# Two banks for value products, filler tied to them, and a new order of pools in the running streams' stage

## The chip, the cores and the metric

The kernel runs on one core of one Trainium2 chip, in one launch. The metric is the device time of that launch in microseconds (us); a profiled execution gives the trace. The engines run side by side, each in its own fixed order: PE (TensorE, matmuls and transposes), ACT (ScalarE), DVE (VectorE), POOL (GpSimd), and SP, which issues the DMA transfers.

## The reference

One inference step of a one-layer streaming encoder, for one prompt of 1024 frames with 16 meta rows ahead of it, and for 8 running streams of 16 new frames each, over shared weights. Attention with 16 heads of 64 and a state-space branch run in parallel, are merged by gates, and a convolutional feed-forward layer follows. The attention is "stick-breaking", and it is what the changed stage computes:

```python
def stick_breaking(q, k, v, q_pos, k_pos):
    z = jnp.einsum('bqhd,bshd->bhqs', q, k).astype(jnp.float32) * (SB_HEAD_DIM ** -0.5)
    reach = k_pos[None, :] < q_pos[:, None]
    log_beta = jax.nn.log_sigmoid(z)
    log_keep = jnp.where(reach, jax.nn.log_sigmoid(-z), 0.0)
    later = lax.cumsum(log_keep, axis=3, reverse=True) - log_keep
    w = jnp.where(reach, jnp.exp(log_beta + later), 0.0)
    return jnp.einsum('bhqs,bshd->bqhd', w.astype(v.dtype), v)
```

A running stream attends to 272 cached positions (16 meta rows and 256 past frames) and its own 16. All is float32.

## The kernel before, in words

Activations lie transposed, channels on partitions. A float32 product is made of three matmuls on numbers split into a high and a low part (high x high, high x low, low x high); the split is a cast on ACT and a subtraction on DVE. The stages run one after another: norm and projections, the state-space branch, the prompt's attention (`phase_att`), the running streams' attention (`phase_smp`, the stage that changes), the merge, the feed-forward layer.

*Prompt attention.* `head` (L678) runs once per head, 0 to 15. Per head, SP loads the keys' halves `KH` and `KL` (L686, L687) and the queries `QS` (L688, L689) from tiles in memory; each of these names is a ring of two buffers, so the loads of a head can go out while the one before it is at work. PE makes the scores (z, L707 and L710), ACT the sigmoid, DVE the scan, PE transposes the weights and multiplies them with the values (L731, L732), and L739 and L743 finish and store.

*The two first rows.* Queries 0 and 1 of the prompt see at most 16 keys. `first_queries` (L746) does them for all heads at once, from a load of its own (L752 to L755), with small matmuls at L767 and L784, at the beginning of `phase_smp`, in slots of that stage's rings.

*The running streams.* `sample_att` (L790) has 8 streams of two halves (8 heads each): 16 iterations. Ahead of them it loads queries (`qhs`, `qls`), key extensions (`kxh`, `kxl`, 16 transfers, L801) and the last cached rows (`last`, L807). In an iteration: 8 transposes of the cached keys into two banks of `pk`, split into `Ksh` and `Ksl`; POOL puts the new keys and the queries of the stream beside them (L848, L851; the queries in block-diagonal tiles `qdh` and `qdl`, of which there are two sets, used in turn); 12 matmuls make the scores z (L867, L870, L871); ACT makes the sigmoid (L873), POOL the masking (L874) and the complement (L876), DVE the scan (L877) and the products with what is kept (L880, L881); 3 transposes turn the weights, which are split into `wTh` and `wTl`; 9 matmuls (L890 to L892) multiply them with the values (`Vsh`, `Vsl`, and `V3h`, `V3l` for the last rows) into the bank `o`; ACT copies that to `od` (L894); 4 transposes turn it back into a bank `pd`, and ACT copies it out (L902).

*The eight accumulation banks* of that stage: two for the projections (`mm`), two `pk`, one `z`, two `wT` (weights and output transposes in turn), one `o`.

*Filler.* Projection blocks that nothing waits for until the merge are kept back in a list, `fill`: queries, keys and values of later heads and the 16 gate blocks (three tiles of 24 matmuls, 72 in a block; L115, L118, L119). `paced` (L954) ties the first matmul of each tile of a block to a *mark*, a matmul of the stage that has to be issued ahead of it on PE. In the prompt's attention the marks are the scores of every other block of queries; in the stage they are the first z matmul of each iteration. Of the 9 blocks that are left when attention ends, `RESERVE` are kept for the beginning of the merge.

*Order.* Memory pools are entered in a written order, each at the address that follows the one before, so a pool's place in the list decides which pools of the earlier stage lay there, and a tile's first writer waits for the last user of that space. The order of instructions on each engine is set by the framework's list scheduler when the program is built; the engines then run it as it stands, and a semaphore holds an instruction until what it needs is there.

## Time and profile before

| what | before |
|---|---|
| median of 3 runs | 3051.93 us (3051.7 to 3055.76) |
| profiled execution | 3054.39 us, its span 3052.7 us |
| mean granted clock of PE | 0.985 |
| PE busy | 2942.7 us (96%) |
| DVE, ACT, POOL busy | 1803.7 us (59%), 1167.4 us (38%), 632.9 us (21%) |
| prompt attention, about | 900 to 1520 us |
| first z matmul of the streams' stage | 1535.08 us |
| its last output transposes | 1714.44 us |

Times inside a trace are counted from the start of its span. A matmul's row gives its whole duration, and the next one begins before it ends: rates are read from the distances between starts. "Granted clock" is the share of full speed that TensorE was given.

### The profile page before, as it was taken

How to read it: one execution, taken by the hardware profiler on the slowest of the kernel's cores; microseconds unless marked ns; L12 is line 12 of the kernel's file. 1: busy time of each engine (PE TensorE's matmuls, PEld its weight loads, DVE VectorE, ACT ScalarE, POOL GpSimd, SP SyncE). 2: the span in 40 equal slices, each digit the busy share in tenths (PEclk: the TensorE clock that was granted, in tenths of full speed). 3: DMA queues.
4: the chain of work that ended last, by engine and by line, in shares of the span. 5: the costliest groups of instructions: out<-in, count | busy, mean ns of one | idle time of the engine just before them, and what ended most of it. 6: DMA issues, size and time to landing. Idle time of an engine off the chain costs nothing. (4 is left out here: it accounts for less than half of the span.)

```text
span 3052.7 us, 45429 instructions
## 1 busy us (share of the span) xinstructions
PE 2942.7 (96%) x17349; PEld 2795.2 (92%) x17349; DVE 1803.7 (59%) x2945; ACT 1167.4 (38%) x2294; POOL 632.9 (21%) x979
## 2 busy tenths in 40 slices
PE   7999999989998999999899999999999999999998
PEld 6997988979978999999789899999999999999997
DVE  6567677677675777777634441345755454545447
ACT  6432423324234555544434320214534242424245
POOL 0024133142232333333324000002201010101014
PEclk9999999999999999999999999999999999999999
DMA  5435345254465555553444462546211111111113
GB/s 186 110 88 147 106 128 159 79 133 128 129 180 152 167 144 140 161 139 103 78 132 150 140 198 90 149 114 181 80 47 43 43 43 43 43 40 39 43 43 118
DMA packets 445498, 338.46 MB, mean 111 GB/s; under 512 B 43991, under 2 KB 421155, under 8 KB 445279
## 3 DMA queue, kind: packets, MB, share of 16 engines
q1 hardware_dynamic: 445279, 335.54, 38.7%
q8 instruction: 137, 2.24, 0.3%
q14 instruction: 82, 0.67, 0.1%
HBM read 244.31 MB, written 91.15 MB: 110 GB/s over the span
## 5 line engine op out<-in xcount | busy, mean ns | idle before, releaser
L115 PE MATMUL mm<-sh,wh 128*128 128x384 f32 (+3 forms) x2520 | 871.5, 346 | 12.5 <-ACT sh L930 4.4
L118 PE MATMUL mm<-sl,wh 128*128 128x384 f32 (+3 forms) x2520 | 871.0, 346 | 2.4 <-DVE sl L931 1.2
L119 PE MATMUL mm<-sh,wl 128*128 128x384 f32 (+3 forms) x2520 | 867.3, 344 | 0.0
L115 PEld LDWEIGHTS mm<-sh,wh 128*128 128x128 f32 (+1 forms) x2520 | 476.9, 189 | 28.0 <-issue 6.6
L118 PEld LDWEIGHTS mm<-sl,wh 128*128 128x128 f32 (+1 forms) x2520 | 477.7, 190 | 13.2 <-issue 7.0
L119 PEld LDWEIGHTS mm<-sh,wl 128*128 128x128 f32 (+1 forms) x2520 | 477.3, 189 | 7.6 <-issue 5.8
L115 PE MATMUL mm<-ph,wh 128*128 128x386 f32 x1248 | 424.7, 341 | 2.7 <-ACT ph L97 2.0
L118 PE MATMUL mm<-pl,wh 128*128 128x386 f32 x1248 | 424.8, 341 | 0.0
L119 PE MATMUL mm<-ph,wl 128*128 128x386 f32 x1248 | 422.6, 339 | 0.2 <-DVE wl L106 0.2
L106 DVE TENSOR_TENSOR wl<-wf,wh 128x1024 fp32r<-128x1024 f32 (+2 forms) x205 | 255.3, 1246 | 279.0 <-ACT wh L105 278.7
L105 ACT CAST wh<-wf 128x1024 fp32r<-128x1024 f32 (+2 forms) x205 | 212.5, 1037 | 481.4 <-PE mm L118 450.4
L1139 DVE SCALAR_TENSOR_TENSOR acc<-fx,cwf,acc 128x256 f32<-128x256 f32 (+1 forms) x352 | 170.7, 515 | 154.1 <-ACT acc L1137 150.1
L115 PEld LDWEIGHTS mm<-ph,wh 128*128 128x128 f32 x1248 | 236.3, 189 | 3.9 <-ACT ph L97 2.3
L119 PEld LDWEIGHTS mm<-ph,wl 128*128 128x128 f32 x1248 | 236.4, 189 | 0.9 <-DVE wl L106 0.5
L118 PEld LDWEIGHTS mm<-pl,wh 128*128 128x128 f32 x1248 | 235.3, 189 | 1.8
L674 DVE TENSOR_TENSOR_SCAN keep<-keep 128x144 f32<-128x144 f32 (+7 forms) x128 | 179.9, 1408 | 57.5 <-POOL keep L673 56.9
L115 PE MATMUL mm<-ah,wh 128*128 128x384 f32 x528 | 179.9, 341 | 0.0
L119 PE MATMUL mm<-ah,wl 128*128 128x384 f32 x528 | 179.3, 340 | 0.0
L118 PE MATMUL mm<-al,wh 128*128 128x384 f32 x528 | 178.7, 338 | 0.0
L1066 POOL TENSOR_TENSOR sq<-sq,sq 128x386 f32<-128x386 f32 (+1 forms) x42 | 60.2, 1433 | 468.1 <-ACT sq L1065 456.6
L98 DVE TENSOR_TENSOR wTl<-wT,wTh 128x512 fp32r<-128x512 f32 (+3 forms) x176 | 103.0, 602 | 81.2 <-ACT wTh L97 80.4
L1164 DVE TENSOR_TENSOR h<-mm,h 128x384 f32<-128x384 f32 x144 | 79.7, 555 | 119.8 <-PE mm L119 119.5
(324 smaller groups left out, 4579.0 us busy)
## 6 DMA issues: line engine op xcount, KB each, us to landing
wf<-in_w_in SPq DMA_DIRECT2D x80, 512.0 KB
wf<-in_w_up SPq DMA_DIRECT2D x44, 512.0 KB
t<-s_ac SPq DMA_DIRECT2D x36, 512.0 KB
wf<-in_w_down SPq DMA_DIRECT2D x28, 512.0 KB
wf<-in_w_out SPq DMA_DIRECT2D x24, 512.0 KB
s_y<-x SPq DMA_DIRECT2D x16, 577.0 KB
yt<-s_y SPq DMA_DIRECT2D x16, 577.0 KB
KH<-s_kh SPq DMA_DIRECT2D x32, 260.0 KB
```

What stands on the lines that cost most here:

```text
L98: nc.vector.tensor_tensor(out=l, in0=x, in1=h.bitcast(F32), op=ALU.subtract)
L105: nc.scalar.copy(wh, wf)
L106: nc.vector.tensor_tensor(out=wl, in0=wf, in1=wh.bitcast(F32), op=ALU.subtract)
L115: i = nc.tensor.matmul(p, wh[:, k, :], mh[:, c:c + w], start=s, stop=False)
L118: nc.tensor.matmul(p, wh[:, k, :], ml[:, c:c + w], start=False, stop=False)
L119: nc.tensor.matmul(p, wl[:, k, :], mh[:, c:c + w], start=False, stop=e)
L674: nc.vector.tensor_tensor_scan(out=K[:, ::-1], data0=K[:, ::-1], data1=K[:, ::-1], initial=1.0, op0=ALU.mult, op1=ALU.min)
L1066: nc.gpsimd.tensor_tensor(out=acc[:, :w], in0=acc[:, :w], in1=sq, op=ALU.add)
L1139: nc.vector.scalar_tensor_tensor(out=op, in0=src(q), scalar=w(q), in1=op, op0=ALU.mult, op1=ALU.add)
L1164: self.nc.vector.tensor_tensor(out=h, in0=p, in1=h, op=ALU.add)
```

## The change

1. `RESERVE` is 2 in place of 3: one gate block moves from the merge into the streams' stage.
2. A mark in the stage is the first matmul of the value products in place of the first z matmul.
3. `wT` has one bank in place of two, `o` two in place of one, and the output transposes `pd` take their bank from the ring `pk`.
4. `first_queries` runs in `phase_att`, ahead of head 15, in slots of the rings QS, KH and KL.
5. The pools of the stage are entered in another order, and `norm_rows` (a small sum over rows for the state-space norm) runs ahead of `sample_att`.

```diff
@@ -44,7 +44,7 @@
 PAIRS_AT_START = 1
 PAIRS_AFTER_GROUP = {3: (1,)}
 RATE = 1.17
-RESERVE = 3
+RESERVE = 2
 SAMPLE_AFTER = (2, 4, 6, 8)
 FFN_GROUP = 4
 XW = 3 + TP + 19 * NB
@@ -746,15 +746,15 @@
     def first_queries(self):
 
         nc, ap, pa = self.nc, self.ap, self.pa
-        x = self.tile(ap, [128, 4, 288], F32R, 'Ksh').bitcast(F32).rearrange("p a b -> p (a b)")[:, :288]
+        x = self.tile(ap, [128, TP - T0], F32R, 'QS').bitcast(F32)[:, :288]
         x = x.rearrange("p (i j t) -> p i j t", i=2, j=8)
         for i, (qs, ks) in enumerate(((self.s_qh, self.s_kh), (self.s_ql, self.s_kl))):
             nc.sync.dma_start(x[:, i, :, 0:2], qs[:, 0:2].rearrange("(j p) t -> p j t", p=128))
             nc.sync.dma_start(x[:, i, :, 2:18], ks[:, 0:16].rearrange("(j p) t -> p j t", p=128))
-        v = self.tile(ap, [128, 2, 512], F32R, 'Vsh').bitcast(F32)[:16].rearrange("p a (j c) -> p (a j) c", c=128)
+        v = self.tile(ap, [128, TP], F32R, 'KH').bitcast(F32)[:16, :1024].rearrange("p (j c) -> p j c", c=128)
         nc.sync.dma_start(v, self.s_v[:, 0:16].rearrange("j t c -> t j c"))
         nc.vector.tensor_tensor(out=x[:, 0], in0=x[:, 0], in1=x[:, 1], op=ALU.add)
-        Q = self.tile(ap, [128, 512], F32, 'last', bufs=2)[:, :256].rearrange("p (j c) -> p j c", c=32)
+        Q = self.tile(ap, [128, TP], F32R, 'KL').bitcast(F32)[:, :256].rearrange("p (j c) -> p j c", c=32)
         nc.gpsimd.memset(Q, 0.0)
 
         def diagonal(t, e):
@@ -762,7 +762,7 @@
             return bass.AP(d.tensor, d.offset, [d.ap[0], (34, 8), (16, 2)])
         for e in range(2):
             nc.gpsimd.tensor_copy(diagonal(Q.rearrange("p j c -> p (j c)"), e), x[64 * e:64 * e + 64, 0, :, 0:2])
-        ps = self.tile(pa, [128, 512], F32, 'z')
+        ps = self.tile(pa, [128, 512], F32, 'z', bufs=2)
         for j in range(8):
             nc.tensor.matmul(ps[:32, :16], Q[:, j], x[:, 0, j, 2:18], start=(j == 0), stop=(j == 7))
         B = self.tile(ap, [32, 2, 16], F32, 'fb', bufs=1)
@@ -779,7 +779,7 @@
         self.T_(pt[:16, :32], B)
         w = self.tile(ap, [16, 32], F32, 'fw', bufs=1)
         nc.scalar.copy(w, pt[:16, :32])
-        po = self.tile(pa, [128, 512], F32, 'o')
+        po = self.tile(pa, [128, 512], F32, 'o', bufs=2)
         for j in range(8):
             nc.tensor.matmul(po[:, 32 * j:32 * j + 32], v[:, j], w, start=True, stop=True)
         out = self.tile(ap, [128, 8, 2], F32, 'fo', bufs=1)
@@ -864,9 +864,7 @@
                 z = ps[:, 0:288]
                 for j in range(4):
                     qh, ql = (Q[x][:, 128 * j:128 * j + 128] for x in range(2))
-                    mk = nc.tensor.matmul(z, qh, Kh[:, j], start=(j == 0), stop=False)
-                    if j == 0:
-                        marks.append(mk)
+                    nc.tensor.matmul(z, qh, Kh[:, j], start=(j == 0), stop=False)
                     nc.tensor.matmul(z, qh, Kl[:, j], start=False, stop=False)
                     nc.tensor.matmul(z, ql, Kh[:, j], start=False, stop=(j == 3))
                 B = self.tile(ap, [128, 288], F32, 'beta')
@@ -879,20 +877,22 @@
                 w = w3[hf][:, 96 - 32 * (b % 4):224 - 32 * (b % 4)]
                 nc.vector.tensor_tensor(out=w3[hf][:, 96:127], in0=B[:, 256:287], in1=K[:, 257:288], op=ALU.mult)
                 nc.vector.tensor_tensor(out=B[:, :256], in0=B[:, :256], in1=K[:, 1:257], op=ALU.mult)
-                pt = self.tile(pa, [128, 512], F32, 'wT', bufs=2)
+                pt = self.tile(pa, [128, 512], F32, 'wT')
                 for i, x in enumerate((B[:, 0:128], B[:, 128:256], w)):
                     self.T_(pt[:, 128 * i:128 * i + 128], x)
                 wh, wl = (self.tile(ap, [128, 3, 128], F32R, n) for n in ('wTh', 'wTl'))
                 self.split(wh, wl, pt[:, 0:384].rearrange("p (i c) -> p i c", c=128))
-                po = self.tile(pa, [128, 512], F32, 'o')
+                po = self.tile(pa, [128, 512], F32, 'o', bufs=2)
                 vs = [(Vh[:, 0], Vl[:, 0]), (Vh[:, 1], Vl[:, 1]), V3[hf]]
                 for i, (vh, vl) in enumerate(vs):
-                    nc.tensor.matmul(po, wh[:, i], vh, start=(i == 0), stop=False)
+                    mk = nc.tensor.matmul(po, wh[:, i], vh, start=(i == 0), stop=False)
+                    if i == 0:
+                        marks.append(mk)
                     nc.tensor.matmul(po, wh[:, i], vl, start=False, stop=False)
                     nc.tensor.matmul(po, wl[:, i], vh, start=False, stop=(i == 2))
                 od = self.tile(ap, [128, 512], F32, 'od', bufs=1)
                 nc.scalar.copy(od, po)
-                pd = self.tile(pa, [128, 512], F32, 'wT', bufs=2)
+                pd = self.tile(pa, [128, 512], F32, 'pk', bufs=2)
                 for j in range(4):
                     self.T_(pd[:, 128 * j:128 * j + 128], od[:, 128 * j:128 * j + 128])
                 for e in range(2):
@@ -962,7 +962,7 @@
     def phase_att(self, right, rx):
         with ExitStack() as c1:
             self.ap = {n: self.pool(c1, "att_" + n, 2) for n in (
-                'wTh', 'wTl', 'wf32', 'att', 'vf', 'KH', 'KL', 'QS', 'VV', 'keep', *(f'beta{i}' for i in range(8)))}
+                'wTh', 'wTl', 'wf32', 'att', 'vf', 'KH', 'KL', 'QS', 'VV', 'keep', *(f'beta{i}' for i in range(8)), 'fb', 'fw', 'fo')}
             self.pa = self.pool(c1, "att_ps", 1, space=PSUM)
             first = PAIRS_AT_START + sum(len(v) for v in PAIRS_AFTER_GROUP.values())
             self.fill = [b for p in range(first, 8) for b in self.qkv(p, self.pa, 'o')]
@@ -974,6 +974,8 @@
                 self.nc.sync.dma_start(v[:, 0:8], vs[0:1024].rearrange("(j t) d -> t j d", t=128))
                 self.nc.sync.dma_start(v[:16, 8], vs[1024:TP])
                 for e in range(2):
+                    if p == 7 and e == 1:
+                        self.first_queries()
                     marks += self.head(2 * p + e, v[:, :, 64 * e:64 * e + 64])
                     done = self.paced(marks, done, RATE)
                     if p + e == 0:
@@ -985,16 +987,15 @@
 
     def phase_smp(self):
         with ExitStack() as c2:
-            mp = self.stp = self.pool(c2, "mixst", 3)
+
             self.ap = {n: self.pool(c2, "smpa_" + n, 2) for n in (
-                'aout', 'od', 'wTh', 'wTl', 'keep', 'beta', 'v', 'r', 'newton', 'qdh0', 'qhs', 'qls', 'kxh', 'kxl',
-                'last', 'V3h', 'V3l', 'qdl0', 'qdh1', 'qdl1', 'Ksh', 'Ksl', 'Vsh', 'Vsl',
-                'w30', 'w31', 'fb', 'fw', 'fo')}
+                'kxh', 'kxl', 'qhs', 'qls', 'qdh0', 'qdl0', 'qdh1', 'qdl1', 'Ksh', 'Ksl', 'last', 'V3h', 'V3l', 'v', 'r', 'newton',
+                'beta', 'keep', 'Vsh', 'Vsl', 'w30', 'w31', 'wTh', 'wTl', 'od', 'aout')}
+            self.stp = self.pool(c2, "mixst", 3)
             self.pa = self.pool(c2, "smp_ps", 1, space=PSUM)
             rest, self.fill = self.fill[len(self.fill) - RESERVE:], self.fill[:len(self.fill) - RESERVE]
-            self.first_queries()
+            self.norm_rows(self.ap)
             self.sample_att(3 * len(self.fill) / 16)
-            self.norm_rows(self.ap)
             assert not self.fill
             self.fill = rest
```

Line numbers in the profile shift a little: the z matmuls' second and third lines are L868 and L869 in the changed kernel, the first of the value products L888.

What this does to the order is seen at three places. The first is PE in the stage, before, between two iterations: z of one, weights and output of the ones before it, products.

```order
L135 MATMUL pk_16866<-ident_60,ck_16854 128x128 x4
L135 MATMUL wT_16520<-ident_60,od_16518 128x128 x4
L135 MATMUL wT_16579<-ident_60,beta_16571 128x128 x2
L135 MATMUL wT_16579<-ident_60,w_2936_16001 128x128
...
L867 MATMUL z_16806<-Ksh_16779,qdh_2932_15993 128x288
L870 MATMUL z_16806<-Ksl_16780,qdh_2932_15993 128x288
L871 MATMUL z_16806<-Ksh_16779,qdl_2933_15994 128x288
L135 MATMUL pk_16873<-ident_60,ck_16854 128x128 x4
L890 MATMUL o_16587<-Vsh_16553,wTh_16583 128x512
L891 MATMUL o_16587<-Vsl_16554,wTh_16583 128x512
L892 MATMUL o_16587<-Vsh_16553,wTl_16584 128x512
```

The rows of z in two groups, `pk` of the next keys and `wT` of earlier outputs and weights lie between each other: scores and keys of later iterations (z_16806, pk_16873) stand ahead of the products of an earlier one (o_16587).

The same engine with the change, from the end of one iteration's scores to its products, and from these to the next one's scores:

```order
L868 MATMUL z_16247<-Ksl_16221,qdh_2938_16011 128x288
L869 MATMUL z_16247<-Ksh_16220,qdl_2939_16012 128x288
L135 MATMUL wT_16268<-ident_60,beta_16260 128x128 x2
L135 MATMUL wT_16268<-ident_60,w_2941_16018 128x128
L888 MATMUL o_16276<-Vsh_16242,wTh_16272 128x512
L891 MATMUL o_16276<-Vsl_16243,wTh_16272 128x512
L892 MATMUL o_16276<-Vsh_16242,wTl_16273 128x512
```

```order
L892 MATMUL o_16276<-V3h_16043,wTl_16273 128x512
L135 MATMUL pk_16288<-ident_60,od_16286 128x128 x4
L135 MATMUL pk_16307<-ident_60,ck_16295 128x128 x4
L135 MATMUL pk_16314<-ident_60,ck_16295 128x128 x4
L867 MATMUL z_16326<-Ksh_16299,qdh_2936_16009 128x288
```

The weights now follow their own scores directly, the products the weights; the output transposes (pk_16288) stand ahead of the next keys, which take the same ring, and the next scores behind both. Gate blocks stand in 7 of the 16 iterations, all of them behind the first products (17 matmuls between the second and the third product, 25 ahead of the output transposes, 30 behind these, or nearly so).

The second place is POOL in the stage, with the change:

```order
L874 TENSOR_SCALAR keep_16342<-beta_16339 128x288
L862 TENSOR_TENSOR Vsl_16570<-ck_16545,Vsh_16569 128x512
L851 CAST qdh_2938_16011<-qhs_15943 64x4x16 x2
L848 CAST Ksl_16717<-kxl_15948 128x4x32
L848 CAST Ksh_16716<-kxh_15947 128x4x32
L851 CAST qdl_2939_16012<-qls_15944 64x4x16 x2
L872 TENSOR_TENSOR beta_16508<-beta_16508,cst_67 128x16
L874 TENSOR_SCALAR keep_16511<-beta_16508 128x288
```

The copies for a later iteration (L851, L848), into tiles that the scores at work read, stand ahead of this iteration's masking (L872, which was L874).

The third is SP, where head 15's loads go out, before:

```order
L743 DMA s_att_86<-att_14435 64x512
L686 DMA KH_15414<-s_kh_76 64x1040
L687 DMA KL_15415<-s_kl_77 64x1040
L659 DMA s_gate_87<-st_14967 128x386
L686 DMA KH_15414<-s_kh_76 64x1040
L687 DMA KL_15415<-s_kl_77 64x1040
L688 DMA QS_15416<-s_qh_79 64x1026
L689 DMA QS_15416<-s_ql_80 64x1026
```

and with the change:

```order
L743 DMA s_att_86<-att_14885 64x512
L659 DMA s_gate_87<-st_15392 128x384
L686 DMA KH_15467<-s_kh_76 64x1040
L687 DMA KL_15468<-s_kl_77 64x1040
L686 DMA KH_15467<-s_kh_76 64x1040
L687 DMA KL_15468<-s_kl_77 64x1040
L659 DMA s_gate_87<-st_15420 128x386
L688 DMA QS_15469<-s_qh_79 64x1026
L689 DMA QS_15469<-s_ql_80 64x1026
```

The loads of KH, KL and QS stand behind a later attention store (att_14885, two stores on from att_14435); and they take the buffers that head 14 uses, since the two first rows now have the others.

## The prediction

> **What bounds the kernel now.** The first view is the page's table of busy time, with its slices and its costliest groups:
>
> ```profile
> PE 2942.7 (96%) x17349; PEld 2795.2 (92%) x17349; DVE 1803.7 (59%) x2945; ACT 1167.4 (38%) x2294; POOL 632.9 (21%) x979
> L115 PE MATMUL mm<-sh,wh 128*128 128x384 f32 (+3 forms) x2520 | 871.5, 346 | 12.5 <-ACT sh L930 4.4
> ```
>
> TensorE is busy for 96% of the span, and no other engine for more than 59%. So time can be gained only where PE idles or runs at a lower clock, and lost wherever PE is made to wait. The second view is the table of windows around the streams' stage (after the window its length, then busy us and instructions of PE, PEld, DVE, ACT and POOL, then the granted clock, DMA share and GB/s):
>
> ```profile
> 1500.00:1520.00 20.00, 13.43 (x58) 9.75 (x59) 11.03 (x14) 5.68 (x11) 4.27 (x7) 0.74 0.90 113
> 1520.00:1540.00 20.00, 11.95 (x62) 11.09 (x62) 6.87 (x21) 8.46 (x20) 7.98 (x17) 0.59 0.47 105
> 1560.00:1700.00 140.00, 135.16 (x836) 127.85 (x835) 59.54 (x101) 62.12 (x127) 50.64 (x113) 1.00 0.42 133
> 1700.00:1720.00 20.00, 15.22 (x71) 11.76 (x70) 4.08 (x6) 7.28 (x15) 1.77 (x3) 0.91 0.31 78
> 1720.00:1740.00 20.00, 20.00 (x115) 20.00 (x114) 11.21 (x9) 7.44 (x9) 0.00 (x0) 1.00 0.66 194
> ```
>
> Two places are slack: the 40 us across the border from prompt attention to the stage, and the stage's last 20 us. Between them PE works 97% of the time at full clock: there the stage is as short as its PE work. The last row also gives the filler's price: 115 matmuls in 20 us, 0.174 us each, so 12.5 us for a gate block of 72. The third view is PE's timeline at the two ends of the stage (start, duration, instruction, idle time before it and what ended that):
>
> ```profile
> 1520.00 0.68 PE L767 MATMUL z<-Ksh,last 128*32 128x16 f32 x16
> 1528.33 0.20 PE L135 MATMUL wT<-ident,fb 32*16 32x32 f32 x1 [6.93 <-DVE fb L777]
> 1528.80 3.62 PE L784 MATMUL o<-fw,Vsh 16*128 16x32 f32 x16 [0.27 <-ACT fw L781]
> 1532.35 1.11 PE L135 MATMUL pk<-ident,last 128*128 128x128 f32 x4
> 1535.08 0.58 PE L867 MATMUL z<-Ksh,qdh 128*128 128x288 f32 x1 [0.77 <-ACT Ksh L97]
> ...
> 1714.44 0.66 PE L135 MATMUL wT<-ident,od 128*128 128x128 f32 x4 [1.69 <-ACT od L894]
> ```
>
> The two first rows take from 1520.00 to 1532.35, 12.35 us. The stage proper runs from the first z at 1535.08 to the end of the last od transposes at 1715.1: 180 us for 16 iterations and 6 gate blocks.
>
> **The change: the order of PE.** In the new order each iteration runs alone: key transposes, z, weight transposes, value products, output transposes, and only then the next one's. Before, the next iteration's keys and z stood between a z and its weights, or filler did. Now nothing does, because the output transposes have moved to the ring `pk` of the keys: an iteration takes three turns of two slots, so the second key transposes of the next one wait for these output transposes and their copies. The filler cannot step in, since it waits for the first value product. So the latency of the chain counts, which the end of the stage shows today, where filler has run out:
>
> ```profile
> 1698.67 0.30 PE L867 MATMUL z<-Ksh,qdh 128*128 128x288 f32 x1
> 1698.95 0.29 PE L871 MATMUL z<-Ksh,qdl 128*128 128x288 f32 x1
> 1699.73 0.40 PE L890 MATMUL o<-Vsh,wTh 128*128 128x512 f32 x1
> 1700.89 0.39 PE L892 MATMUL o<-V3h,wTl 128*128 128x512 f32 x1
> 1702.26 0.66 PE L135 MATMUL wT<-ident,od 128*128 128x128 f32 x4 [0.98 <-ACT od L894]
> 1702.97 0.27 PE L135 MATMUL wT<-ident,w 128*128 128x128 f32 x1
> 1703.93 0.50 PE L890 MATMUL o<-Vsh,wTh 128*128 128x512 f32 x1 [0.69 <-ACT wTh L97]
> 1705.11 0.63 PE L890 MATMUL o<-Vsh,wTh 128*128 128x512 f32 x1
> 1707.25 0.63 PE L892 MATMUL o<-V3h,wTl 128*128 128x512 f32 x1
> ```
>
> An iteration's eight key transposes in the full flow of the stage:
>
> ```profile
> 1552.38 1.04 PE L135 MATMUL pk<-ident,ck 128*128 128x128 f32 x8
> ```
>
> The rest of the chain, on the other engines:
>
> ```profile
> 1699.32 0.41 ACT L873 ACTIVATE beta<-z 128x288 f32<-128x288 f32 x1 [1.53 <-issue]
> 1702.95 0.42 ACT L902 COPY aout<-wT 64x64 f32<-64x64 f32 x2 [0.75 <-PE wT L135]
> 1699.81 0.22 POOL L874 TENSOR_TENSOR beta<-beta,cst 128x16 f32<-128x16 f32 x1 [1.71 <-ACT beta L873]
> 1700.12 0.43 POOL L876 TENSOR_SCALAR keep<-beta 128x288 f32<-128x288 f32 x1
> 1700.59 0.76 DVE L877 TENSOR_TENSOR_SCAN keep<-keep 128x288 f32<-128x288 f32 x1 [0.81 <-POOL keep L876]
> 1701.56 0.42 DVE L881 TENSOR_TENSOR beta<-beta,keep 128x256 f32<-128x256 f32 x1
> ```
>
> Z ends at 1699.24; sigmoid, masking, complement, scan and product end at 1701.98. The gap from z to the weights is 2.8 us. Then 0.7 us from the weights to the first product (the cast), 1.0 us from the last product to the output transposes (the copy), 0.75 us to the copies that free `pk`, and 0.75 us for the keys' cast ahead of z (0.77 at 1535.08): gaps of 6.0 us. PE's own work is 9 products at 0.23 (five steps in 1.16 us), 12 z at 0.14, 8 + 4 + 3 transposes at 0.12 (eight in 1.04, with the last one's end): 5.6 us, of which the first four key transposes (0.5) fall into a gap. 6.0 + 5.1 makes a **period of about 11.0 us** without filler, where the stage today hides all but PE's own work.
>
> POOL can lengthen it. In its new order six copies for a later iteration stand ahead of the masking, and they wait for this very z's last matmuls:
>
> ```profile
> L851 POOL CAST qdh<-qhs 64x64 fp32r<-64x64 f32 x28 | 7.6, 273 | 36.2 <-PE z L870 35.4
> L848 POOL CAST Ksh<-kxh 128x128 fp32r<-128x128 f32 x14 | 4.2, 302 | 0.9 <-PE z L871 0.9
> ```
>
> Two of the first and one of the second for the high halves, and as many for the low ones, are 1.7 us, of which the sigmoid and its hand-over (0.6) run beside: at most 1.1 us more, period 12.1 us. I take half, 11.6.
>
> Seven iterations carry a gate block behind the first value products, which fills the gap to the output transposes and that to the copies (1.75 us): a block adds 12.5 - 1.75 = 10.8 us. Sum of the stage at full clock: 16 x 11.6 + 7 x 10.8 = 186 + 76 = 262 us; bounds 252 and 270.
>
> **The clock.** The trace shows how little rest lowers it (windows of 2 us, the clock in the third column from the end):
>
> ```profile
> 1504.00:1506.00 2.00, 0.00 (x0) 0.00 (x0) 1.90 (x2) 0.00 (x0) 0.00 (x0) 1.00 0.97 91
> 1506.00:1508.00 2.00, 0.85 (x3) 0.45 (x3) 1.41 (x3) 0.80 (x2) 1.09 (x3) 0.61 1.11 104
> 1508.00:1510.00 2.00, 2.00 (x5) 1.26 (x6) 1.10 (x2) 0.27 (x1) 0.00 (x0) 0.50 0.96 106
> 1540.00:1542.00 2.00, 2.00 (x14) 1.97 (x13) 0.69 (x1) 0.86 (x2) 0.00 (x0) 0.86 0.61 208
> ```
>
> A rest of some 3 us before 1506.7 halves it, and after 1535.08 it takes 5 us of matmuls to come back (0.86 in the window from 1540). At 1705.11 to 1707.25 the products stand 0.43 us apart (five steps in 2.14), nearly double. In the new order the stretch from z to the first product is 2.8 + 0.3 + 0.7 = 3.8 us with 0.3 us of work in it (4.4 with half of the copies), and an iteration without filler has nowhere 5 us of unbroken work. So the nine without filler should run at half clock: products +1.75, z +0.55, transposes +0.85, by these rows +3.1 us each, 28 us. Those with a block start it at half clock: z, keys, weights and the first filler, about +1.5 us, 10 us. Stage 262 + 38 = 300 us; bounds 252 (no penalty, no copies) and 270 + 46 = 316 (all sixteen lose somewhat more). The change to today's 180: **+120 us**, from +72 to +136.
>
> The Trainium skill, TensorE: Matmul & The Clock Gate, section Part 1: The HAM clock gate, has the array at half clock after one idle window of about 3.4 us and back after one busy window of that length, the windows running free. By it about half of the 38 us would be lost. The rows from 1703.93 to 1707.25 speak for the dearer reading: nearly half clock there with no idle of 3.4 us ahead.
>
> **The change at head 15.** The two first rows now take slots of the rings of QS, KH and KL, so the loads for head 15 wait until head 14's last z has read its own:
>
> ```profile
> 1430.55 0.46 SPq L686 DMA_DIRECT2D KH<-s_kh  x1
> 1434.10 0.59 SPq L689 DMA_DIRECT2D QS<-s_ql  x1
> 1468.72 0.32 PE L707 MATMUL z<-KH,QS 128*128 128x344 f32 x1
> 1469.92 0.28 PE L707 MATMUL z<-KH,QS 128*128 128x256 f32 x1
> DMA packets 1573, 2.36 MB, mean 197 GB/s; under 512 B 133, under 2 KB 1127, under 8 KB 1572
> ```
>
> Today they are issued 35 us before use. Now they go out after 1469.2, with head 15's first z due at 1469.92. They are 4 x 260 + 2 x 256.5 KB = 1.55 MB, 7.9 us at the 197 GB/s measured over 1429 to 1441 (the last row), 9 us with the issues: z near 1478. Some 3 us of other PE work stand there, so PE loses 5 us, and 2 more for the rows' own matmuls at full clock: +7. SP's order also has those loads ahead of gate stores and a weight load, which the same 7 us delay; filler already loaded covers that.
>
> **The change at the border.** The gap of 12.35 us for the two first rows goes; that is the gain. Against it: the key extensions and query loads wait for the end of the attention's tail, and SP then issues 8 of the former, 2 queries, 16 key tails and 16 value tails, at 0.46 to 0.60 each (rows of the loads above) some 20 us in a row; the filler now waits for the first value product, one chain later. From 1520.00 the first z stood 15.1 us off, and filler began behind it; I estimate 17 us to z and 25 to the first product. Net from -12 (gain kept whole) to +10; I take +2.
>
> **Sum of squares moved ahead.** norm_rows' few instructions fall beside the tail; on ACT and DVE they cost 0 to 1.6 us there, inside the bounds above. The merge begins with one gate block less: -12.5 us, if the loads behind it are not waited for instead. ACT's scaled rows already end 4.4 us of PE's waits (the group of L115); a shorter cover gives back 0 to 12.5. I take 6.
>
> **Sum.** 3054.39 (the profiled execution, 2.46 above the median shown) + 120 + 7 + 2 - 6 = 3177; less 2 for the median: 3175. Between the outer bounds: low 3052 + 72 + 5 - 12 - 12.5 = 3104; high 3052 + 136 + 8 + 10 = 3206.
>
> **Rivals.** (1a) The chain is serial, but a gap of 3.8 us lowers the clock only now and then: half of the 38 us, 3156. For it: the 3 us that halved it before 1506.7 were wholly idle, and here 0.3 us of work stands in the gap. (1b) The clock holds throughout: 3137. For it: blocks of 12.5 us of full work in 7 of 16 iterations. Against both: the slow products from 1703.93 on. (2) The order costs nothing in the stage, because what I read as a wait is covered; then only the edges count: 7 + 2 - 6, and 12.5 for the added block, 3067. Against it: no instruction stands between a z and its weights in the new order, and PE runs in order. (3) **Not slower**: the gap at the border is gained whole and the period is short. With the block (7 x 10.8 = 76), +7 and -6 and -12.35, today's time is reached at 16 P = 180 + 11 - 76, P = 7.2 us; below that it is faster. At 5.0 us, PE's own work, the time would be 3052 - (7.2 - 5.0) x 16 = 3017, at 6.5 some 3041; between them 3030. It would take z to weights in under 1 us or z ahead of the products; the sigmoid, scan and product alone take 1.6.
>
> **Numbers.** Forecast 0.45; rival 1a 0.22, 1b 0.17; rival 2 0.07; rival 3 0.05; above the high bound (the stage's loads late besides) 0.04. Range 3108 to 3206, which takes in 1a and 1b and leaves out the last three, and what lies at the edges of the first three. What the measurement can tell from no change is 0.2%, 6 us: faster 0.04, same 0.03 (rival 3 near its point, or rival 2 with the outer gains), slower 0.93.
>
> **What would show it.** Right: from first z to the last od transposes about 300 us; PE's idle put before `wT<-ident,beta` (waiting for DVE's L881 product) of 2.5 to 4 us, sixteen times; clock 0.5 to 0.7 in windows without filler; no filler between a z and its products; head 15's first z waiting for the DMA of KH, KL or QS some 5 us. Wrong: a stage under 230 us; idle put before filler rows instead (then weight loads are late); a clock of 1.0 throughout (1b); a merge that starts with PE idle over 6 us (then the reserve was its cover).

## The result and the profile after

The changed kernel takes 3190.08 us (median of 4 runs, 3188.48 to 3195.04) where the kernel before takes 3051.81 us beside it: a ratio of 1.0456, with a 95% interval of 1.0443 to 1.0469. It is 138 us slower; 3175 was forecast, with a range of 3108 to 3206. The profiled execution has a span of 3189.7 us, 137.0 us more than before's 3052.7, and the clock granted over it is 0.964 where it was 0.985.

The page of the changed kernel, busy time and slices:

```profile
PE 2994.4 (94%) x17349; PEld 2826.8 (89%) x17349; DVE 1805.1 (57%) x2945; ACT 1170.6 (37%) x2294; POOL 630.1 (20%) x979
PE   7999999999999999998677789999999999999998
...
PEclk9999999999999999998778789999999999999999
```

PE runs the same 17349 matmuls, for 52 us longer. The loss lies in one place: slices 19 to 23 (counted from 0), where both PE and its clock sink, are the streams' stage. The windows of the stage, from its first z to its last od transposes, say how (after the window its length, busy time and instructions of PE, PEld, DVE, ACT and POOL, the clock, DMA share, GB/s). Before:

```profile
1535.00:1715.00 180.00, 169.18 (x1005) 157.55 (x1006) 72.60 (x123) 77.35 (x156) 57.76 (x133) 0.98 0.42 131
```

and with the change:

```profile
1545.60:1868.50 322.90, 232.56 (x1077) 199.04 (x1078) 75.71 (x125) 82.53 (x160) 56.16 (x132) 0.80 0.27 82
```

The stage grew from 180 to 322.9 us, by 143. PE's idle time in it went from 10.8 to 90.3 us, which is 79.5 of these; its busy time rose by 63.4, of which 12.5 are the added gate block and the rest is work at a lower clock, 0.80 where it was 0.98. Who waits there is told by the view of waits over the same stretch of the changed kernel (total, times, longest, in us):

```profile
POOL qdh L851 <- PE z L868: 104.3, 14, 13.2
PE wT L135 <- DVE beta L879: 60.6, 16, 4.4
DVE keep L875 <- POOL keep L874: 57.0, 16, 4.4
```

PE's transposes of the weights wait for DVE's product in all 16 iterations, 60.6 us in all. In the same view of the kernel before, over its stage, this wait does not stand at all, and the longest of PE's waits is

```profile
PE wT L135 <- ACT od L894: 3.4, 3, 1.7
```

PE's timeline in the changed kernel: the first weights of the stage, and the last two iterations, the first of them behind a block (rows that only go on with the same tiles are left out):

```profile
1554.84 0.66 PE L135 MATMUL wT<-ident,beta 128*128 128x128 f32 x2 [4.38 <-DVE beta L879]
...
1842.23 0.37 PE L867 MATMUL z<-Ksh,qdh 128*128 128x288 f32 x1 [1.04 <-ACT Ksh L97]
1845.24 0.44 PE L869 MATMUL z<-Ksh,qdl 128*128 128x288 f32 x1
1848.57 0.66 PE L135 MATMUL wT<-ident,beta 128*128 128x128 f32 x2 [2.88 <-DVE beta L879]
1850.01 0.80 PE L888 MATMUL o<-Vsh,wTh 128*128 128x512 f32 x1 [0.57 <-ACT wTh L97]
1854.89 0.66 PE L135 MATMUL pk<-ident,od 128*128 128x128 f32 x4 [0.73 <-ACT od L894]
1855.39 1.33 PE L135 MATMUL pk<-ident,ck 128*128 128x128 f32 x8
1856.77 0.37 PE L867 MATMUL z<-Ksh,qdh 128*128 128x288 f32 x1
1858.84 0.29 PE L869 MATMUL z<-Ksh,qdl 128*128 128x288 f32 x1
1862.02 0.41 PE L135 MATMUL wT<-ident,beta 128*128 128x128 f32 x2 [2.89 <-DVE beta L879]
1867.37 1.12 PE L135 MATMUL pk<-ident,od 128*128 128x128 f32 x4 [0.73 <-ACT od L894]
```

Each iteration is a chain with nothing of another in it. From weights to weights an iteration without filler takes 14.5 us on average, one with a block 27.3 (eight and seven of them make the 307.2 us from 1554.84 to 1862.02).

At the border, four of PE's rows in the changed kernel:

```profile
1476.27 0.58 PE L707 MATMUL z<-KH,QS 128*128 128x256 f32 x1 [1.57 <-DMA QS<-s_ql]
1526.29 0.64 PE L739 MATMUL o<-wf,VV 128*128 128x144 f32 x4
1539.26 1.09 PE L135 MATMUL pk<-ident,last 128*128 128x128 f32 x4 [12.34 <-DMA last<-in_cache_k]
1545.62 0.58 PE L867 MATMUL z<-Ksh,qdh 128*128 128x288 f32 x1 [0.77 <-ACT Ksh L97]
```

Head 15's first scores come at 1476.27, 6.35 us later than before; the tail ends at 1526.9 (before 1520.1) and the first z is 10.5 us later. The 12.35 us that the two first rows held PE are replaced by a wait of 12.34 us for the last cached rows, and behind it PE waits 2.56 us more for the values of these rows. From the stage's end to that of the span it is 1321.2 us where it was 1337.6. So 6.9 + 3.6 + 142.9 - 16.4 = 137.0.

### The profile page after: what moved, and what is told of

It reads as the page before. It is cut to its first block, busy times and chain, and to the rows that moved or that the text cites. A ratio compares the mean times of both kernels' runs of the same rounds, so it can differ in the third digit from the quotient of the medians.

```text
span 3189.7 us, 45521 instructions
## 1 busy us (share of the span) xinstructions
PE 2994.4 (94%) x17349; PEld 2826.8 (89%) x17349; DVE 1805.1 (57%) x2945; ACT 1170.6 (37%) x2294; POOL 630.1 (20%) x979
## 4 chain that ended last, share of the span: by engine, by line
PE 74%; DMA 7%; DVE 7%; issue 6%; POOL 3%; ACT 2%; SPq 1%; POOLq 0%; ACTq 0%; DVEq 0%
PE mm L115 21%; PE mm L118 20%; PE mm L119 20%; PE wT L135 3%; DMA t<-s_ac 2%; DMA yt<-s_y 1%; PE z L707 1%; DVE t L458 1%; DMA zf<-s_z 1%; PE o L732 1%; PE z L710 1%; PE o L731 1%; PE yd L472 1%; PE tp L135 1%; POOL Vsl L862 1%
## 5 line engine op out<-in xcount | busy, mean ns | idle before, releaser
L115 PE MATMUL mm<-sh,wh 128*128 128x384 f32 (+3 forms) x2520 | 872.5, 347 | 7.6 <-DVE st L549 2.3
L115 PEld LDWEIGHTS mm<-sh,wh 128*128 128x128 f32 (+1 forms) x2520 | 479.3, 190 | 23.1 <-issue 6.6
L115 PE MATMUL mm<-ph,wh 128*128 128x386 f32 x1248 | 425.2, 341 | 2.0 <-ACT ph L97 2.0
L115 PEld LDWEIGHTS mm<-ph,wh 128*128 128x128 f32 x1248 | 236.8, 190 | 2.9 <-ACT ph L97 2.3
L135 PE MATMUL wT<-ident,beta 128*128 128x128 f32 x736 | 123.6, 282 | 65.8 <-DVE beta L879 60.6
L115 PE MATMUL mm<-ah,wh 128*128 128x384 f32 x528 | 179.8, 340 | 0.0
L135 PEld LDWEIGHTS wT<-ident,beta 128*128 128x128 f32 x736 | 94.4, 147 | 81.5 <-issue 62.2
```

What stands on the lines that cost most here:

```text
L115: i = nc.tensor.matmul(p, wh[:, k, :], mh[:, c:c + w], start=s, stop=False)
L135: self.nc.tensor.transpose(out, in_, self.ident[:k, :k])
```

## The experiments

The theory (A): the output transposes in the ring of the keys make the iterations run one at a time. The rival (B): the marks do it, since filler tied to the value products cannot fill the gap ahead of them. Four kernels separate the two edits, each alone on the kernel before, and each undone in the changed one. These four, and the last two kernels of this section, were run once each; runs of the kernel before lie between 3046 and 3057 us. The lengths of stages are read from one trace of each kernel.

**The banks alone.** On the kernel before:

```diff
-                pt = self.tile(pa, [128, 512], F32, 'wT', bufs=2)
+                pt = self.tile(pa, [128, 512], F32, 'wT')
-                po = self.tile(pa, [128, 512], F32, 'o')
+                po = self.tile(pa, [128, 512], F32, 'o', bufs=2)
-                pd = self.tile(pa, [128, 512], F32, 'wT', bufs=2)
+                pd = self.tile(pa, [128, 512], F32, 'pk', bufs=2)
```

> The kernel before with the third edit alone: one bank for the weights' transposes, two for the value products, the output transposes in the ring of the key transposes. Theory A (the ring makes each iteration run alone): PE's order is serial; the ten iterations without filler take some 14 us each as in the changed kernel, the six with a block some 20, since its 45 matmuls stand in the gap from the scores to the weights: stage 260 us where it was 180, time 3125 to 3145. Theory B (the marks, not the banks, open the gap): the time stays within 10 us of before.

Measured: 3133.74 us beside 3052.75, stage 263.2 us. PE's first rows in the view of waits:

```profile
PE wT L135 <- DVE beta L881: 37.1, 10, 3.9
PE pk L135 <- ACT od L894: 13.4, 16, 1.0
```

The gap is open in exactly the 10 iterations that have no block; in the other 6 the filler closes it. This edit alone makes 83 us of the stage's loss.

**The marks alone.** On the kernel before, `marks.append` moved from the first z matmul to the first value product.

> The kernel before with the second edit alone: filler is tied to the first value product. Theory A: the next scores still run ahead and fill the gap, so the stage stays under 205 us and the time rises by 5 to 25 us, 3057 to 3077. Theory B (the marks open the gap): the stage is over 260 us, the time over 3130.

Measured: 3063.41 us beside 3052.75, stage 188.4 us. With the rings as before, the next keys and scores run ahead and fill the gap, so filler is hardly missed.

**The banks undone** in the changed kernel (`wT` two, `o` one, `pd` in `wT`):

> The changed kernel with the third edit undone (two banks for weights and output transposes in turn, one for value products); all else as changed. Theory A: nearly all of the stage's loss goes; stage 193 (its 180 and a block of 12.5) to 215 us, time 3050 to 3080. Theory B: the stage stays over 290 us, time over 3155.

Measured: 3068.74 us, stage 201.2 us. Of 143 us of loss in the stage, 122 go.

**The marks undone** in the changed kernel:

> The changed kernel with the second edit undone: filler is tied to the first z matmul again. Theory A: the order stays serial; seven gaps are filled by 45 matmuls of a block, nine stay open; 9 x 14.5 + 7 x 20 = 270 us for the stage where it is 323, time some 3135 (3125 to 3150). Theory B: the stage returns to some 193 us, the time to 3060.

Measured: 3131.77 us, stage 268.5 us: 54 us go, since seven gaps are filled again. The four results agree with A, and rule out B as the whole cause. But the two edits cost more together than the sum of both: banks alone +83 us in the stage, marks alone +8, both +143, of which 12.5 are the added block. What closes a gap today is either the next scores or filler; the one edit takes away the first, the other the second.

**What is left without the two.** The changed kernel with both undone:

> The changed kernel with the second and third edits undone (banks and marks as before); what is left is the moved gate block, the two first rows ahead of head 15, and the pools. Theory A (the two undone edits made the stage's loss): stage 190 to 197 us, first z as late as in the changed kernel (+10 us), the rest 16 us shorter; 3050 to 3066. Theory B (pools and late head also hold the stage back, by POOL's copies or late loads): stage over 205, time over 3070.

Measured: 3056.58 us, ratio to before 1.0015 (1.0006 to 1.0024), stage 188.5 us, a little under the range of theory A. It is 8.5 us longer than before with 12.5 us of work more in it.

**Two banks without the keys' ring.** The changed kernel with marks as before and

```diff
-                pd = self.tile(pa, [128, 512], F32, 'pk', bufs=2)
+                pd = self.tile(pa, [128, 512], F32, 'o', bufs=2)
```

> The changed kernel with the marks at the first z again and the output transposes in the ring of the value products (two banks) in place of the keys' ring. Theory A: with the keys' ring free the next scores run ahead, so two banks for products are no harm: stage 188 to 200 us, 3048 to 3066. Theory B (sharing any ring with the output transposes makes the iterations run alone): stage over 240, time over 3110.

Measured: 3053.21 us, ratio 1.0002 (0.9992 to 1.0011), stage 187.6 us. The kernel with the marks undone differs from this one in the ring of `pd` alone, and its stage takes 268.5 us, 81 more. So neither two banks for the products nor a shared ring as such is the fault: the output transposes stand at the end of an iteration and the keys at its beginning, and sharing a ring between these two ties the beginning of the next iteration to the end of this one.

**The two first rows alone**, moved ahead of head 15, on the kernel before:

> The kernel before with the fourth edit alone: the two first rows ahead of head 15. Theory A: head 15 begins 6 to 8 us late since its loads wait for head 14's last scores, and the 12 us between the tail and the keys' tails are saved only in part: first z between -6 and +5 us, time 3046 to 3058. Theory B (the gap is gained whole): first z 12 us earlier, time under 3043.

Measured: 3048.75 us, ratio 0.9989 (0.9979 to 0.9998), the only one of these kernels that beats the kernel before, by a tenth of a per cent, with the end of the interval close to 1. First z 5.5 us later, just past the edge of what theory A allows, but the stage is 173.8 us, 6.2 less, and the rest 3.0 less. Why the stage is shorter is not shown.

**The gate block alone** (`RESERVE` 2 on the kernel before):

> The kernel before with the first edit alone: one gate block of the merge goes into the stage. Theory A: the stage grows by a block's 12.5 us or less, the rest shrinks by the 16 us seen in the changed kernel: 3044 to 3051. Theory B (the block was the cover of the merge's loads): the rest shrinks by less than 9 us, time 3052 to 3062.

Measured: 3054.29 us, ratio 1.0006 (0.9996 to 1.0015). The stage is 9.7 us longer and the rest 6.6 us shorter: theory B. PE's waits behind the stage, from 1715 to 1800:

```profile
PE mm L115 <- ACT sh L930: 7.0, 3, 3.6
```

It was 4.4 us before. Of the block's 12.5 us the merge gains only 6.6, so about half of it had been a cover there; the longer wait is 2.6 us of the 5.9 that are not gained, and where the others went is not shown. But then the 16.4 us of the changed kernel need another reason.

**norm_rows alone**, put ahead of the streams' attention, on the kernel before:

```diff
-            self.sample_att(3 * len(self.fill) / 16)
             self.norm_rows(self.ap)
+            self.sample_att(3 * len(self.fill) / 16)
```

> The kernel before with norm_rows alone put ahead of the streams' attention (a part of the fifth edit; no pool moved). Theory A: the merge's scaled rows wait for norm_rows' result, so the rest after the stage shrinks by the 5 to 11 us by which the changed kernel's gain there exceeds that of the block alone; stage unchanged; 3041 to 3048. Theory B (that gain came from the later begin of the merge, which gave the loads time): within 4 us of before.

Measured: 3050.36 us, ratio 1.0 (0.9991 to 1.0009); the rest is 1337.8 us, as before. Theory A is wrong here. Seen over the kernels, the rest after the stage goes with something else: 1331.0 and 1331.3 us where the reserve is 2 and the pools are as before, 1320 to 1323 in all seven with the reserve at 2 and the new order of pools. SP's rows show what the pools do. Before, the merge's first loads are issued 1 us after the stage's last transposes (1715.1):

```profile
1716.06 0.52 SPq L924 DMA_DIRECT2D rB<-s_rs  x1
1721.39 0.81 SPq L927 DMA_DIRECT2D yt<-s_y  x2
```

in the changed kernel 49 us ahead of them (1868.5):

```profile
1819.42 0.34 SPq L924 DMA_DIRECT2D rB<-s_rs  x1
1819.82 0.90 SPq L927 DMA_DIRECT2D yt<-s_y  x2
```

The merge's tiles lie where the stage's first pools were. With the new order these are the key extensions and queries, which are done with early, so the loads start inside the stage, and the wait for ACT's scaled rows is gone from the changed kernel. Two kernels differ in the order of pools alone: the one with two banks without the keys' ring has the new order, the combination below has the old one. PE's wait at L115 behind the stage, first with the old order, then with the new:

```profile
PE mm L115 <- ACT sh L930: 7.6, 4, 4.0
PE mm L115 <- ACT sh L930: 0.4, 2, 0.2
```

The rest is 1331.3 us with the old order and 1320.4 with the new, so the pools do shorten the merge by 10.9 us. But the same pair shows what they cost earlier: the stage is 181.4 us with the old order and 187.6 with the new, and from the attention's tail to the first z it is 16.2 and 18.6 us. Most of the gain is given back, and both kernels take the time of the kernel before (ratio 1.0002 each). Why the stage grows with the new order is not shown.

**A combination.** On the kernel before: the reserve at 2, the first rows ahead of head 15, norm_rows ahead, `pd` in the ring of the products (two banks, and one for the weights); pools and marks as before.

> The kernel before with edits one and four, norm_rows ahead, two banks for value products with the output transposes in their ring; marks and pools as before. If the parts add up: -3 (first rows) +2 (block) -8 (norm_rows) -1 (banks), 3038 to 3046. If the parts cover the same waits: 3046 to 3053.

Measured: 3053.42 us, ratio 1.0002 (0.9993 to 1.001). That is just above both ranges. norm_rows, counted at -8, gives nothing, as the run of it alone has it; the first rows (-3) and the block (+2), as they were measured alone, come to -1 us with it, and the interval here runs from -2 to +3, so nothing is left to explain.

**The gap filled with useless work.** The changed kernel with 24 transposes of the identity after each iteration's scores, into an unused quarter of the weights' bank (they compute nothing that is used):

```diff
                 pt = self.tile(pa, [128, 512], F32, 'wT')
+                for i in range(24):
+                    du = nc.tensor.transpose(pt[:, 384:512], self.ident, self.ident)
+                    if i == 0:
+                        self.issue_after(du, mz)
```

(`mz` is the last matmul of the scores.)

> The changed kernel with 24 transposes of the identity matrix, whose result nothing reads, after each iteration's scores: 2.7 us of PE work at full clock, 4.0 at half, in a gap of 3.85 us. Theory C (the open gaps keep PE at half clock, and that is worth 38 us or a little more): clock in the stage near 1.0 where it was 0.80, time 25 to 45 us less, 3145 to 3165. Theory D (the clock costs little; the rest of the gap over my sum is the chain): within 10 us of 3190.

Measured: 3157.06 us, 33 us faster with 384 instructions more. The stage's window:

```profile
1540.40:1833.20 292.80, 245.99 (x1462) 218.61 (x1463) 75.65 (x125) 81.99 (x159) 56.05 (x132) 0.96 0.29 90
```

The clock is 0.96 where it was 0.80 and the stage 30 us shorter: theory C. The price of the clock is at least these 30 us; behind four of the seven blocks some of the scores still run at half clock there. The dummies are transposes, so transposes too count as work for this clock.

**The masking on DVE.** The changed kernel with the two POOL instructions of the chain (L872, L874) on DVE:

```diff
-                nc.gpsimd.tensor_tensor(out=B[:, 272:288], in0=B[:, 272:288], in1=self.late, op=ALU.mult)
+                nc.vector.tensor_tensor(out=B[:, 272:288], in0=B[:, 272:288], in1=self.late, op=ALU.mult)
-                nc.gpsimd.tensor_scalar(out=K, in0=B, scalar1=-1.0, scalar2=1.0, op0=ALU.mult, op1=ALU.add)
+                nc.vector.tensor_scalar(out=K, in0=B, scalar1=-1.0, scalar2=1.0, op0=ALU.mult, op1=ALU.add)
```

> The changed kernel with masking and complement of the streams' stage on DVE in place of POOL, so that POOL's copies stand ahead of nothing in the chain. Theory E (the copies lengthen the gap by 1.0 us in 14 iterations): gap from 3.85 to 2.9 us or less, stage 13 to 25 us shorter, time 3165 to 3178. Theory F (they are covered by the sigmoid; the gap is the chain's own): the time stays within 6 us of 3190.

Measured: 3174.03 us, stage 301.7 us, 21 less. PE's wait:

```profile
PE wT L135 <- DVE beta L879: 41.5, 16, 3.3
```

60.6 us became 41.5, 1.2 us an iteration. Two things went at once, the copies ahead of the chain and a hand-over between engines. The changed kernel itself parts them: its last two iterations have no copies for a later one, and their gaps are 2.88 and 2.89 us where most of the others are 3.8 to 3.9. On POOL one of the others looks so:

```profile
1592.96 0.53 POOL L851 CAST qdh<-qhs 64x64 fp32r<-64x64 f32 x2 [3.06 <-PE z L868]
1594.03 0.52 POOL L851 CAST qdl<-qls 64x64 fp32r<-64x64 f32 x2
1594.63 0.22 POOL L872 TENSOR_TENSOR beta<-beta,cst 128x16 f32<-128x16 f32 x1
1594.94 0.43 POOL L874 TENSOR_SCALAR keep<-beta 128x288 f32<-128x288 f32 x1
```

So the copies cost 1.0 us in each of 14 iterations, and the hand-over the other 0.3 in each of the 16 (14 x 1.0 + 16 x 0.3 = 19 of the 19.1 us).

## Why the prediction was right, and where it was off

**The serial chain: right.** The order on PE, read from the program, was what the chip ran; the gap stands where it was said, 16 times, of 2.9 to 4.4 us. The stage's idle time came out near the sum: by the prediction's own prices PE works 16 x 5.6 + 7 x 12.5 = 177 us of the 262, which leaves 85 idle; measured 90.3. That is luck in part, for two errors meet there. An iteration without filler idles 5.4 us on average where the sum has 6.1; the key transposes follow the output transposes with at most 0.08 us between them, so the 0.75 us for the copies that free `pk` did not exist on PE. One with a block idles 5.9 us where the sum has 4.35 (6.1 less 1.75). The block does hide the 0.73 us ahead of the output transposes, but ahead of the scores PE waits about 1.57 us (1.04 and 0.53) where an iteration without filler waits 0.3 or less. In all seven the cast of the keys (L97) stands on ACT behind two instructions that the filler brought:

```profile
1840.17 1.05 ACT L105 CAST wh<-wf 128x1024 fp32r<-128x1024 f32 x1 [3.57 <-PE mm L118]
1841.12 0.49 ACT L658 ACTIVATE st<-mm 128x386 f32<-128x386 f32 x1
1841.51 1.06 ACT L97 CAST Ksh<-pk 128x512 fp32r<-128x512 f32 x2
```

So a block hides nothing in sum, where the prediction took 1.75 us.

**PE's own time in the stage: the term that was too small.** The stage (322.9 us) exceeds the 300 forecast by 23 us: 5 are idle time, 18 are PE's busy time, 177 + 38 for the clock = 215 predicted and 232.6 measured. The stage before, at a clock of 0.98, and one block more are 169.2 + 12.5 = 181.7 us of work; the other 51 go with the lower clock, for which 38 was taken. The iterations without filler were met (14.7 predicted, 14.5 measured). Those with a block were not: 11.6 + 10.8 + 1.5 = 23.9 predicted, 27.3 measured, 7 times, 24 us. Of the 3.4 us by which one is longer than predicted, 1.5 are the idle time above; the others are the clock, for which 1.5 us was too little. In the trace the first two products and about half of the 17 filler matmuls behind them still run at half clock (the 17 take 3.9 to 4.4 us where 3.0 was the full rate), and behind the block, after the wait ahead of the scores, 4 to 9 of the 12 scores are at half clock again.

**POOL's copies: the bound, not the middle.** 1.1 us at most was the bound and half of it was taken; 1.0 was measured. These 6 us of idle time more do not show in the sum, since the other waits of the iterations without filler were shorter than summed.

**The clock.** 38 us by rows of before, 51 by the busy time above; the dummies recovered 30 of the stage. The reading by the Trainium skill (TensorE: Matmul & The Clock Gate, Part 1: The HAM clock gate), by which an idle window of about 3.4 us throttles, was put at half of the 38; the trace bears out the length of the window and goes against the need for a wholly idle one, as below.

**Head 15: right.** z at 1476.27 where "near 1478" was said, tail 6.9 us late where 7 was said. In this trace head 14 ran 2.7 us ahead of before's (its last scores begin at 1466.06, before at 1468.72), so head 15 was held up by 9 us, which is what the prediction had for the loads and their issues. PE idles for 3.6 of these, 1.57 for the loads themselves and 2.00 for a cast on DVE ahead of them, where some 5 were expected. That one trace meets the 7 is partly chance, but the size is right: the tail ends between 1514.5 and 1520.1 in the five kernels whose first rows stand where they were, between 1521.7 and 1527.9 in the nine that have them ahead of head 15, and the means are 7.5 us apart.

**The border: the sign right, the size near.** +3.6 us beyond the tail, +2 predicted. The queue of small loads on SP took the place of the 12.35 us. The first z varies between 1540.4 and 1547.2 over seven kernels with the same edits here, but that is the tail's doing: from tail to first z all seven take 18.6 to 19.3 us. The kernels with the first rows where they were take 15.0 to 17.5, and the two with the rows moved and the pools as before 15.9 and 16.2. So moving the rows gains nothing there, and the order of pools costs 2 to 3 us.

**The merge: -16.4 against -6.** The prediction looked at the reserve alone, where its "shorter cover gives back" was right: the block alone gave 6.6 us. What it missed is the pools' new order, which it priced only by what waits at the stage's beginning, and not by what may start at its end: some 10 us gained there, most of which the pools cost in the stage and at the border.

**The sum.** 3177 was predicted for a profiled execution; this one is 3191.44. Stage +23, border and head +1, merge -10 make +14. Two errors of opposite sign made it look better than its largest term was; that the sum is 14 us off and not 23 is luck.

**The rivals.** The clock that recovers (1a and 1b) fell with the clock of 0.80 and with the 30 us and more that it cost; the order that costs nothing (2) and the faster case (3) fell with the period of 14.5 us, where 7.2 was the point.

## What to carry to other kernels

Before two tiles share a ring of buffers, ask where in an iteration each stands: a tile used at the end and one used at the beginning tie the next iteration's start to this one's end, however many buffers other rings are given. Work that overlaps covers for other work that does: here the next scores closed the gap without filler, and in the iterations that had a block the filler closed it without the next scores; removing both cost far more than the two losses apart. And read an order of pools from both sides: what the new owner must wait for at the start, and which loads of the next stage may begin before the end. Here the second gained 10.9 us and the kernel as a whole nothing.

## What the hardware showed that was not expected

The clock falls after much less rest than the prediction's 3 us. Windows of 1 us in the changed kernel, behind a block that had kept PE busy at full clock for over 10 us:

```profile
1840.00:1841.00 1.00, 1.00 (x10) 0.91 (x8) 0.00 (x0) 0.83 (x1) 0.00 (x0) 1.00 0.00 0
1841.00:1842.00 1.00, 0.18 (x2) 0.00 (x0) 0.75 (x1) 1.00 (x4) 0.00 (x0) 1.00 0.00 0
1842.00:1843.00 1.00, 0.37 (x1) 0.19 (x1) 1.00 (x3) 0.57 (x2) 0.00 (x0) 1.00 0.51 190
1843.00:1844.00 1.00, 0.87 (x5) 0.87 (x6) 0.68 (x2) 0.00 (x0) 0.00 (x0) 0.86 0.26 77
1844.00:1845.00 1.00, 1.00 (x6) 1.00 (x5) 0.00 (x0) 0.00 (x0) 0.00 (x0) 0.50 0.92 221
```

Two waits of 1.04 and 0.53 us, with PE busy for 0.55 of 2 us, and the clock halves while the matmuls are already running again. It came back at 1854, after 4 us of unbroken products. So what lowers it looks like the share of busy time over the last few us and not one long rest; that is an inference from these windows, and no run took it apart. The rest of the trace fits it. In the stage the clock changes only on a grid of 3.41 us: it fell at 1843.73 and came back at 1853.97, three steps later. Windows laid on that grid:

```profile
1836.90:1840.31 3.41, 3.41 (x22) 3.37 (x21) 0.00 (x0) 0.14 (x1) 0.00 (x0) 1.00 0.17 60
1840.31:1843.73 3.42, 1.84 (x14) 1.42 (x12) 2.42 (x3) 2.26 (x4) 0.00 (x0) 1.00 0.19 66
1843.73:1847.14 3.41, 1.95 (x9) 1.60 (x7) 0.11 (x1) 0.41 (x1) 0.65 (x2) 0.50 1.03 293
1847.14:1850.55 3.41, 1.42 (x4) 1.00 (x5) 1.73 (x4) 0.48 (x1) 0.00 (x0) 0.50 0.66 162
1850.55:1853.97 3.42, 3.42 (x9) 2.34 (x7) 0.00 (x0) 0.00 (x0) 0.00 (x0) 0.50 0.00 0
1853.97:1857.38 3.41, 2.31 (x14) 1.47 (x13) 0.69 (x2) 2.17 (x5) 0.00 (x0) 1.00 0.00 0
```

From 1550 us to the end of the stage there are 16 such windows at full clock after which it halved, with PE busy for 0.08 to 0.54 of the window, and 40 after which it held, all at 0.50 or more. At half clock there are 15 after which it came back, all at 0.85 or more, and 22 after which it did not, all at 0.83 or less. So in this stage a window with PE at rest for about half of it lowered the clock, and only one nearly full brought it back; a matmul's end is modelled in the trace, so these shares are rough. The Trainium skill, TensorE: Matmul & The Clock Gate, section A second HAM failure mode: psum-queue depth-cycling, tells of a kernel whose PE idles briefly but often enough for the clock to swing; this trace agrees with that, at waits of 1.6 us in sum.
